# Moving the first layer norm's weight and bias from the residual to the turned tiles

## The chip, the cores and the metric

One core of one Trainium2 chip runs the kernel. The metric is the device time in microseconds (us) of one execution; of several executions the median is given.

## The reference

One decoder layer on 256 tokens of width 2048, all in float32. Three branches are gated, projected and merged; then

```
mix = merged @ w_out
x   = layer_norm(ALPHA * x + mix, ln1_g, ln1_b)
h   = x @ w_up                        # 2048 -> 2 * 5632
...                                   # causal convolution of width 3, silu(a) * b
x   = layer_norm(ALPHA * x + a @ w_down, ln2_g, ln2_b)
```

Only `ln1_g` and `ln1_b`, the weight and bias of the first of these two layer norms, are handled differently by the change.

## The kernel before

Every matrix product runs in three (or, by columns, two) passes: each float32 operand is split into a rounded part ("hi") and a remainder ("lo"). `pieces` streams a weight matrix as 1 MB transfers into two buffers called `raw`, all on the queue of SyncE. A ScalarE copy makes `whi` and a VectorE subtraction makes `wlo`; both live in four staging buffers, and a fifth piece waits until TensorE has finished with the first. `raw` is free again only after the subtraction.

`tok_major` computes tokens by columns. For each of the 16 row blocks of the weights ("k-tiles") it issues three matmuls for each half of the tokens (128 each). The last 512 columns of `w_out` go another way: KEEP = 14 of the 16 k-tiles go to buffers of their own (`khi`, `klo`), are first used for token half 0 alone, and are then gone through again for token half 1. Between those matmuls the first layer norm of half 0 is worked in. `wout_done` is called when a half is complete, and `wout_during` before the end of the second pass, at the moments when `left` k-tiles are still to come.

The layer norm of one half: `ln1_stats` adds the residual and takes mean and variance (VectorE, then a power on GpSimd). `ln1_norm` normalises 512 columns on ScalarE; `ln1_scale` multiplies by the weight on VectorE and adds the bias on GpSimd, with both vectors spread over all partitions in the tile `gb1` (2 MB of transfers); `ln1_fused` does normalisation, weight and bias in two VectorE instructions. `ln1_turn` transposes four 128 x 128 blocks on TensorE into one of two PSUM buffers `ax`, ScalarE copies them as the hi part into `x1T`, and `ln1_low` subtracts on VectorE for the lo part. `x1T` is what the up-projection multiplies, and `x1` keeps the finished rows as the residual for the second layer norm.

The first block of the up-projection, `feat_major_halves`, also runs by token halves. It uses four pieces that `pull()` has fetched beforehand (`up_kept`, two transfers of 1 MB), and calls `between` (`ln1_rest`) ahead of each, where the transposes of half 1 are issued.

TensorE's order is that of the source in the whole kernel. On ScalarE and VectorE a planner of the compiler sets the order from priorities (`hp`) and its own idea of when inputs are there, except inside `ordered`, where these two engines follow the source. Where instructions from outside that region fall between those inside is again the planner's. Each engine then works strictly in the order it was given.

`rstd_of` ends with `nmr`, minus the mean times the reciprocal deviation: one VectorE and one GpSimd instruction. After the up-projection the buffers `x1T0` and `x1T1` are used again: the first for `g2`, weight and bias of the second layer norm, the second for `spare`, a home for two of the last pieces of `w_down`.

The columns `l1g` and `l1b` (weight and bias with one feature per partition) are made at the start of the kernel, in both versions.

Of the kernel before, what the change touches and what calls it, by code (L numbers as in the profile page):

```python
# [8 lines left out]
F32 = mybir.dt.float32  # L9
F32R = mybir.dt.float32r  # L10
U8 = mybir.dt.uint8
AF = mybir.ActivationFunctionType
ALU = mybir.AluOpType
# [3 lines left out]
P = 128  # L17
S = 256
NT = S // P
D = 2048  # L20
KD = D // P
# [9 lines left out]
LEVELS = (64, 32, 16, 8, 4, 2, 1)  # L31
RAW_BUFS = 2
XPAD = 24
KEEP = 14
ENDS = (256, 512)
CROSS = 5
STARTS = ((0, 2), (2, 2), (4, 4), (8, 4), (12, 4))
# [4 lines left out]
def hybrid_layer(  # L42
# [6 lines left out]
    nc = tc.nc  # L49
    ctx.enter_context(tc.manual_schedule(engines={ENG.PE}))  # L50
    x2 = x[0]
    win, wup, wout, wdown = w_in[0], w_up[0], w_out[0], w_down[0]
# [4 lines left out]
    def sub(o, a, b):  # L57
        nc.vector.tensor_tensor(out=o, in0=a, in1=b, op=ALU.subtract)  # L58

    def add(o, a, b):  # L60
        nc.vector.tensor_tensor(out=o, in0=a, in1=b, op=ALU.add)  # L61

    def mul(o, a, b):
        nc.vector.tensor_tensor(out=o, in0=a, in1=b, op=ALU.mult)  # L64

    def stt(o, a, s, b, op0, op1):
        nc.vector.scalar_tensor_tensor(out=o, in0=a, scalar=s, in1=b, op0=op0, op1=op1)  # L67

    def act(o, a, f, **kw):
        nc.scalar.activation(out=o, in_=a, func=f, **kw)  # L70
# [10 lines left out]
    def pieces(w2, col, width, kt_n, big, step, home=None, low=lambda k0: nc.vector):  # L81
        wv = w2.rearrange("(k p) c -> p k c", p=P)
        for b0 in range(0, kt_n, big):
            bn = min(big, kt_n - b0)
            with hp():
                raw = wst.tile([P, bn, width], F32, name="raw", bufs=RAW_BUFS)
                nc.sync.dma_start(out=raw, in_=wv[:, b0:b0 + bn, col:col + width])
            for s0 in range(0, bn, step):
                n = min(step, bn - s0)
                with hp():  # L90
                    hi, lo = (home or stage)(b0 + s0, n, width)
                    split(hi, lo, raw[:, s0:s0 + n, :], low(b0 + s0))
                yield b0 + s0, n, hi, lo
# [115 lines left out]
    def rstd_of(pool, st, want_nmr=True):  # L209
        mv = pool.tile([P, 4], F32, name="ln_mv", bufs=2)  # L210
        nc.vector.bn_aggr(out=mv[:, 0:2], in_=st)  # L211
        nc.vector.tensor_scalar(out=mv[:, 1:2], in0=mv[:, 1:2], scalar1=LN_EPS, scalar2=None, op0=ALU.add)
        nc.gpsimd.tensor_tensor(out=mv[:, 1:2], in0=mv[:, 1:2], in1=mhalf_c, op=ALU.pow)
        if want_nmr:
            nc.vector.tensor_scalar(out=mv[:, 2:3], in0=mv[:, 0:1], scalar1=-1.0, scalar2=None, op0=ALU.mult)
            nc.gpsimd.tensor_tensor(out=mv[:, 2:3], in0=mv[:, 2:3], in1=mv[:, 1:2], op=ALU.mult)
        return mv[:, 0:1], mv[:, 1:2], mv[:, 2:3]

    xpool_cm = tc.tile_pool(name="xpool", bufs=1, side="right", reuse_waits="tile")
# [31 lines left out]
    def bc(t, n):  # L251
        return t.rearrange("p (a b) -> p a b", b=n)
# [85 lines left out]
    tp = ax_tile()  # L338
    nc.tensor.transpose(tp[:, 0:56], vrow, ident[0:56, 0:56])
    nc.vector.tensor_copy(out=vcol, in_=tp[:, 0:56])  # L340
    lbh, normg, pscale, l1g, l1b = (vcol[:, a:b] for a, b in ((0, 8), (8, 16), (16, 24), (24, 40), (40, 56)))
# [19 lines left out]
    for g in range(2):  # L361
        tp = bc(ax_tile(), P)
# [10 lines left out]
    for j in range(2):  # L373
        ps = tok_major(win, 6144 + 512 * j, xT, KD)
# [3 lines left out]
    for t in range(NT):  # L378
# [3 lines left out]
        _, rs, nmr = rstd_of(mix, st)  # L382
# [5 lines left out]
    for j in range(4):  # L388
# [3 lines left out]
        tp = ax_tile()  # L392
# [34 lines left out]
    for j in range(4):  # L427
        ps = feat_major(win, 5120 + 256 * j, xT, KD)
# [259 lines left out]
    ff = ff_cm.__enter__()  # L688
    x1T_h = [ff.tile([P, KD // 2, 2 * S], F32R, name=f"x1T{i}") for i in range(2)]
    x1 = ff.tile([P, NT, D], F32, name="x1")  # L690
    st1 = ff.tile([P, NT, 4, 6], F32, name="st1")
    for j in range(4):
        cs = slice(512 * j, 512 * (j + 1))
# [2 lines left out]
    keep_cm = tc.tile_pool(name="keep", bufs=KEEP // 2, reuse_waits="tile")  # L696
    keep = keep_cm.__enter__()

    gb1 = keep.tile([P, 2, D], F32, name="gb1", bufs=1)
    nc.gpsimd.dma_start(out=gb1[:, 0, :], in_=ln1_g[0].partition_broadcast(P))  # L700
    nc.gpsimd.dma_start(out=gb1[:, 1, :], in_=ln1_b[0].partition_broadcast(P))

    def keep_home(k0, n, width):
        if k0 < KD - KEEP:
            return stage(k0, n, width)
# [2 lines left out]
    ln1_mr = {}  # L708
    ln1_tp = {}

    def ln1_stats(t, ps):
        cs = slice(1536, 2048)
        stt(x1[:, t, cs], x1[:, t, cs], ALPHA, ps, ALU.mult, ALU.add)
        nc.vector.bn_stats(out=st1[:, t, 3, :], in_=x1[:, t, cs])
        ln1_mr[t] = rstd_of(ff, st1[:, t])

    def ln1_fused(t, c):
        mu, rs, _ = ln1_mr[t]
        cs = slice(512 * c, 512 * (c + 1))
        xc = x1[:, t, cs]  # L720
        stt(xc, xc, mu, gb1[:, 0, cs], ALU.subtract, ALU.mult)
        stt(xc, xc, rs, gb1[:, 1, cs], ALU.mult, ALU.add)

    def ln1_norm(t, c):
        _, rs, nmr = ln1_mr[t]
        xc = x1[:, t, 512 * c:512 * (c + 1)]
        act(xc, xc, AF.Identity, scale=rs, bias=nmr)

    def ln1_scale(t, c):
        cs = slice(512 * c, 512 * (c + 1))  # L730
        xc = x1[:, t, cs]
        mul(xc, xc, gb1[:, 0, cs])
        nc.gpsimd.tensor_tensor(out=xc, in0=xc, in1=gb1[:, 1, cs], op=ALU.add)  # L733

    def ln1_turn(t, c):
        tp = bc(ax_tile(), P)
        for j in range(4):
            nc.tensor.transpose(tp[:, j, :], x1[:, t, 512 * c + j * P:512 * c + (j + 1) * P], ident)  # L738
        xh, c4 = x1T_h[c // 2], 4 * (c % 2)
        hi = xh[:, c4:c4 + 4, t * P:(t + 1) * P]  # L740
        act(hi, tp, AF.Copy)
        ln1_tp[t, c] = xh[:, c4:c4 + 4, S + t * P:S + (t + 1) * P], tp, hi.bitcast(F32)

    def ln1_low(t, c):
        sub(*ln1_tp[t, c])

    for j in range(3):
        cs = slice(512 * j, 512 * (j + 1))
        ps = tok_major(wout, 512 * j, mT, KD) if j else first_out
        with hp():  # L750
            for t in range(NT):
                stt(x1[:, t, cs], x1[:, t, cs], ALPHA, ps[t], ALU.mult, ALU.add)
                nc.vector.bn_stats(out=st1[:, t, j, :], in_=x1[:, t, cs])
    up_pieces = pieces(wup, 0, 256, KD, 8, 4, low=lambda k0: nc.vector if k0 < 8 else nc.gpsimd)
    up_kept = []
    up_next = pieces(wup, DFF, 256, KD, 8, 4)
    up_early = []

    def pull():
        up_kept.append(next(up_pieces))  # L760

    ordered = tc.manual_schedule(engines={ENG.Activation, ENG.DVE})

    def wout_done(t, ps, c0, c1):
        with hp(2):
            if t == 0:
                ordered.__enter__()
                ln1_stats(0, ps)
                pull()
                for c in range(4):  # L770
                    ln1_norm(0, c)
                    ln1_scale(0, c)
                pull()
            else:
                ln1_stats(1, ps)
                pull()
                ln1_low(0, 2)
                ln1_low(0, 3)
                ln1_norm(1, 2)
                ln1_norm(1, 3)  # L780
                ln1_fused(1, 0)
                ln1_fused(1, 1)

    def wout_during(c):
        with hp(2):
            ln1_turn(0, c)
            if 0 < c < 3:
                ln1_low(0, c - 1)
            if c == 2:
                pull()  # L790

    tok_major(wout, 1536, mT, KD, last=KEEP, home=keep_home, done=wout_done,
              during={left: [lambda c=c: wout_during(c)] for c, left in enumerate((5, 3, 2, 0))})

    def x1T(k):
        return x1T_h[k // 8][:, k % 8, :]

    def ln1_rest(t, c):
        with hp(2):
            if (t, c) == (0, 3):  # L800
                ln1_turn(1, 0)
                ln1_scale(1, 2)
                ln1_low(1, 0)
                ln1_scale(1, 3)
            elif (t, c) == (1, 0):
                ln1_turn(1, 1)
                ln1_low(1, 1)
            elif (t, c) == (1, 1):
                ln1_turn(1, 2)
                ln1_low(1, 2)  # L810
                ln1_turn(1, 3)
                ln1_low(1, 3)
                up_early.append(next(up_next))
            elif (t, c) == (1, 2):
                up_early.append(next(up_next))
                ordered.__exit__(None, None, None)

    ps_first = feat_major_halves(up_kept, x1T, KD, ln1_rest)
    keep_cm.__exit__(None, None, None)
# [6 lines left out]
    for j in range(KF // 2):  # L826
        ac = []
        for half in range(2):
            if j == 0 and half == 0:
                ps = ps_first  # L830
# [20 lines left out]

    st2 = up.tile([P, NT, 5, 6], F32, name="st2", bufs=1)
    g2 = ff.tile([P, 2, D], F32, name="x1T0")
    spare = ff.tile([P, 2, 4, 512], F32R, name="x1T1")

    def tail_home(k0, n, width):
        if 32 <= k0 < 36:
# [49 lines left out]
    for j in range(3):  # L907
        cs = slice(512 * j, 512 * (j + 1))
        ps = tok_major(wdown, 512 * j, aT, KF)
        if j == 0:  # L910
            nc.gpsimd.dma_start(out=g2[:, 0, :], in_=ln2_g[0].partition_broadcast(P))
            nc.gpsimd.dma_start(out=g2[:, 1, :], in_=ln2_b[0].partition_broadcast(P))
        with hp():
            for t in range(NT):
                stt(x1[:, t, cs], x1[:, t, cs], ALPHA, ps[t], ALU.mult, ALU.add)
                nc.vector.bn_stats(out=st2[:, t, j, :], in_=x1[:, t, cs])
    tok_major(wdown, 1536, aT, KF, last=12, home=tail_home, done=ln2_last, ends=ENDS)
    up_cm.__exit__(None, None, None)
    ff_cm.__exit__(None, None, None)
# [40 lines left out]
```

## Time and profile before

| | |
|---|---|
| median of three runs | 1600.36 us (1599.52 to 1601.9) |
| the profiled execution's own time | 1600.03 us |
| its span, first to last instruction | 1598.3 us |
| TensorE busy | 1578.2 us |
| VectorE, ScalarE, GpSimd busy | 1001.7, 828.8, 48.4 us |
| read from memory | 301.71 MB |
| mean granted TensorE clock | 0.997 of full |

The 1.7 us between span and time lie before the first and after the last instruction. TensorE is busy nearly throughout, so a change moves the time by what TensorE waits, or by the clock it is granted.

### The profile page before, as it was taken

The page shows a single profiled execution, that of the slowest core. Times are in us where ns is not written, and L with a number is a line of the kernel's source. Part 1 is how long each engine was busy: PE and PEld are TensorE (multiplying, and loading weights), DVE is VectorE, ACT ScalarE, POOL GpSimd, SP SyncE. Part 2 cuts the span into 40 slices and gives each one's busy share as a digit, 9 for nine tenths or more (in the row PEclk, how much of TensorE's full clock was granted, in tenths as well). Part 3 has the DMA queues.
Part 4 walks back from the last instruction along what each step waited for, and adds up shares of the span by engine and source line. Part 5 has one row for each costly group of instructions (what it writes and reads, how often), then busy time and mean ns, then how long its engine had stood idle before and what let it go on. Part 6 is the DMA issues. An engine that isn't in the chain of part 4 may idle for free. (4 is left out here: it accounts for less than half of the span.)

```text
span 1598.3 us, 20294 instructions
## 1 busy us (share of the span) xinstructions
PE 1578.2 (99%) x8129; PEld 1344.8 (84%) x8129; DVE 1001.7 (63%) x1196; ACT 828.8 (52%) x962; POOL 48.4 (3%) x116
## 2 busy tenths in 40 slices
PE   9999999999999999999999999999999999999997
PEld 7888888888888887888888888888888888888886
DVE  6666547765448755447567677676676667445455
ACT  5455558546458555444435555555555555333332
POOL 1100000000000001000003000000000000000001
PEclk9999999999999999999999999999999999999999
DMA  7656555655555547655553655555655556655553
GB/s 246 234 185 198 185 191 174 195 178 169 192 189 172 199 160 263 211 186 183 187 208 106 210 186 184 186 191 194 193 184 185 187 192 231 208 185 201 193 186 130
DMA packets 217213, 305.10 MB, mean 191 GB/s; under 512 B 5148, under 2 KB 137812, under 8 KB 216608
## 3 DMA queue, kind: packets, MB, share of 16 engines
q1 hardware_dynamic: 214912, 294.67, 55.8%
q0 software_dynamic: 2208, 9.16, 1.7%
q8 instruction: 63, 1.03, 0.3%
q14 instruction: 30, 0.25, 0.0%
HBM read 301.71 MB, written 2.10 MB: 190 GB/s over the span
## 5 line engine op out<-in xcount | busy, mean ns | idle before, releaser
L74 DVE TENSOR_TENSOR wlo<-raw,whi 128x1024 fp32r<-128x1024 f32 x541 | 659.1, 1222 | 530.4 <-ACT whi L70 529.7
L70 ACT ACTIVATE whi<-raw 128x1024 fp32r<-128x1024 f32 x543 | 571.1, 1056 | 664.2 <-PE mm L151 281.6
L108 PE MATMUL mm<-x1T,whi 128*128 128x512 f32 x1376 | 432.2, 395 | 0.0
L111 PEld LDWEIGHTS mm<-x1T,wlo 128*128 128x128 f32 x1376 | 258.5, 188 | 61.1
L111 PE MATMUL mm<-x1T,wlo 128*128 128x256 f32 x1376 | 270.3, 278 | 0.0
L150 PE MATMUL mm<-wlo,X 128*128 128x512 f32 x612 | 238.4, 389 | 1.3 <-DVE wlo L74 1.3
L149 PE MATMUL mm<-whi,X 128*128 128x512 f32 x612 | 239.5, 391 | 0.0
L151 PE MATMUL mm<-whi,X 128*128 128x512 f32 x612 | 238.2, 389 | 0.0
L108 PEld LDWEIGHTS mm<-x1T,whi 128*128 128x128 f32 x1376 | 209.4, 189 | 0.0
L108 PE MATMUL mm<-X,whi 128*128 128x512 f32 x640 | 201.5, 396 | 0.9 <-DVE X L74 0.9
L111 PEld LDWEIGHTS mm<-X,wlo 128*128 128x128 f32 x640 | 120.2, 188 | 28.4
L150 PEld LDWEIGHTS mm<-wlo,X 128*128 128x128 f32 x612 | 114.9, 188 | 25.1 <-DVE wlo L74 2.0
L149 PE MATMUL mm<-whi,aT 128*128 128x512 f32 (+1 forms) x352 | 135.2, 384 | 0.0
L150 PE MATMUL mm<-wlo,aT 128*128 128x512 f32 (+1 forms) x352 | 135.2, 384 | 0.0
L151 PE MATMUL mm<-whi,aT 128*128 128x512 f32 (+1 forms) x352 | 135.2, 384 | 0.0
L151 PEld LDWEIGHTS mm<-whi,X 128*128 128x128 f32 x612 | 114.9, 188 | 24.1
L149 PEld LDWEIGHTS mm<-whi,X 128*128 128x128 f32 x612 | 114.9, 188 | 23.5 <-ACT whi L70 0.2
L111 PE MATMUL mm<-X,wlo 128*128 128x256 f32 x640 | 125.8, 278 | 0.0
L108 PEld LDWEIGHTS mm<-X,whi 128*128 128x128 f32 x640 | 97.7, 189 | 1.5 <-DVE X L74 1.2
L150 PEld LDWEIGHTS mm<-wlo,aT 128*128 128x128 f32 x352 | 66.1, 188 | 13.2
L151 PEld LDWEIGHTS mm<-whi,aT 128*128 128x128 f32 x352 | 66.1, 188 | 13.1
L149 PEld LDWEIGHTS mm<-whi,aT 128*128 128x128 f32 x352 | 66.1, 188 | 13.0
(189 smaller groups left out, 1281.1 us busy)
## 6 DMA issues: line engine op xcount, KB each, us to landing
raw<-in_w_in_dram SPq DMA_DIRECT2D x102, 1024.0 KB, 5.0
raw<-in_w_up_dram SPq DMA_DIRECT2D x88, 1024.0 KB, 5.1
raw<-in_w_down_dram SPq DMA_DIRECT2D x44, 1024.0 KB, 5.0
raw<-in_w_out_dram SPq DMA_DIRECT2D x16, 1024.0 KB, 5.1
raw<-in_w_pool_proj_dram SPq DMA_DIRECT2D x8, 1024.0 KB, 5.0
raw<-in_w_sg_proj_dram SPq DMA_DIRECT2D x8, 1024.0 KB, 5.1
raw<-in_w_hg_proj_dram SPq DMA_DIRECT2D x8, 1024.0 KB, 5.0
x<-in_x_dram POOLq DMA_DIRECT2D x4, 512.0 KB, 7.6
```

What stands on the lines that cost most here:

```text
L70: nc.scalar.activation(out=o, in_=a, func=f, **kw)
L74: low.tensor_tensor(out=lo, in0=src, in1=hi.bitcast(F32), op=ALU.subtract)
L108: nc.tensor.matmul(ps[:, c, :], lhsT=hi[:, k, c * P:(c + 1) * P], rhs=xT(kt)[:, 0:512], start=kt == 0, stop=False)
L111: nc.tensor.matmul(ps[:, c, 0:256], lhsT=lo[:, k, c * P:(c + 1) * P], rhs=xT(kt)[:, 0:256], start=False, stop=kt == kt_n - 1)
L149: nc.tensor.matmul(o[:, w], lhsT=xT(kt)[:, xs], rhs=hi[:, k, w], start=kt == first, stop=False)
L150: nc.tensor.matmul(o[:, w], lhsT=xT(kt)[:, xs], rhs=lo[:, k, w], start=False, stop=False)
L151: nc.tensor.matmul(o[:, w], lhsT=xT(kt)[:, xl], rhs=hi[:, k, w], start=False, stop=kt == kt_n - 1)
```

## The change

- `KEEP` is 16: all k-tiles of the last block of `w_out` are kept, and the first pass serves token half 0 alone from the start. `gb1` no longer lies beside them.
- `ln1_norm` normalises all eight pieces of 512 columns on ScalarE, and `x1` then holds the normalised rows without weight and bias. `ln1_scale` and `ln1_fused` go.
- `ln1_turn` applies weight and bias after the transpose: four ScalarE instructions for the hi part and four VectorE instructions into a new tile `full`, one each per 128 x 128 block, and one subtraction for the lo part. Everything of a turn is emitted together.
- All four `pull()` of the first up block are emitted before `ordered` begins, and all four of their subtractions are VectorE's; two were GpSimd's.
- The turns of half 0 come at 7, 5, 3 and 1 k-tiles left; those of half 1 two at once ahead of the last piece of half 0, then one ahead of each of the first two pieces of half 1.
- `nmr` is one VectorE instruction.
- `gb1` is loaded at the start of the down-projection into `x1T1`, and `x1` is multiplied and added there, 16 VectorE instructions on 128 x 512. `spare` is taken afterwards.

```diff
-KEEP = 14
+KEEP = 16
...
         if want_nmr:
-            nc.vector.tensor_scalar(out=mv[:, 2:3], in0=mv[:, 0:1], scalar1=-1.0, scalar2=None, op0=ALU.mult)
-            nc.gpsimd.tensor_tensor(out=mv[:, 2:3], in0=mv[:, 2:3], in1=mv[:, 1:2], op=ALU.mult)
+            nc.vector.tensor_scalar(out=mv[:, 2:3], in0=mv[:, 0:1], scalar1=mv[:, 1:2], scalar2=-1.0, op0=ALU.mult,
+                                    op1=ALU.mult)
...
-    gb1 = keep.tile([P, 2, D], F32, name="gb1", bufs=1)
-    nc.gpsimd.dma_start(out=gb1[:, 0, :], in_=ln1_g[0].partition_broadcast(P))
-    nc.gpsimd.dma_start(out=gb1[:, 1, :], in_=ln1_b[0].partition_broadcast(P))
...
+        full = bc(keep.tile([P, 512], F32, name="full", bufs=2), P)
+        for j in range(4):
+            k = 4 * c + j
+            g, b = l1g[:, k:k + 1], l1b[:, k:k + 1]
+            act(xh[:, c4 + j, t * P:(t + 1) * P], tp[:, j, :], AF.Identity, scale=g, bias=b)
+            nc.vector.tensor_scalar(out=full[:, j, :], in0=tp[:, j, :], scalar1=g, scalar2=b, op0=ALU.mult, op1=ALU.add)
         hi = xh[:, c4:c4 + 4, t * P:(t + 1) * P]
-        act(hi, tp, AF.Copy)
...
+        sub(xh[:, c4:c4 + 4, S + t * P:S + (t + 1) * P], full, hi.bitcast(F32))
...
-    up_pieces = pieces(wup, 0, 256, KD, 8, 4, low=lambda k0: nc.vector if k0 < 8 else nc.gpsimd)
+    up_pieces = pieces(wup, 0, 256, KD, 8, 4)
...
             if t == 0:
+                for _ in range(4):
+                    pull()
                 ordered.__enter__()
-                ln1_stats(0, ps)
-                pull()
-                for c in range(4):
-                    ln1_norm(0, c)
-                    ln1_scale(0, c)
-                pull()
...
+            ln1_stats(t, ps)
+            for c in range(4):
+                ln1_norm(t, c)
...
-              during={left: [lambda c=c: wout_during(c)] for c, left in enumerate((5, 3, 2, 0))})
+              during={left: [lambda c=c: wout_during(c)] for c, left in enumerate((7, 5, 3, 1))})
...
             if (t, c) == (0, 3):
                 ln1_turn(1, 0)
...
+                ln1_turn(1, 1)
+            elif t == 1 and c < 2:
+                ln1_turn(1, 2 + c)
+            elif t == 1:
                 up_early.append(next(up_next))
...
-    spare = ff.tile([P, 2, 4, 512], F32R, name="x1T1")
+    gb1 = ff.tile([P, 2, D], F32, name="x1T1")
+    nc.gpsimd.dma_start(out=gb1[:, 0, :], in_=ln1_g[0].partition_broadcast(P))
+    nc.gpsimd.dma_start(out=gb1[:, 1, :], in_=ln1_b[0].partition_broadcast(P))
+    for c in range(4):
+        cs = slice(512 * c, 512 * (c + 1))
+        for t in range(NT):
+            mul(x1[:, t, cs], x1[:, t, cs], gb1[:, 0, cs])
+            add(x1[:, t, cs], x1[:, t, cs], gb1[:, 1, cs])
...
+    spare = ff.tile([P, 2, 4, 512], F32R, name="x1T1")
     tok_major(wdown, 1536, aT, KF, last=12, home=tail_home, done=ln2_last, ends=ENDS)
```

## Rows read from the trace of the kernel before

**Rows 1.** First part of the page: busy time, share, instructions.
```profile
PE 1578.2 (99%) x8129; PEld 1344.8 (84%) x8129; DVE 1001.7 (63%) x1196; ACT 828.8 (52%) x962; POOL 48.4 (3%) x116
```

**Rows 2.** Waits of TensorE, whole span: total us, times, longest.
```profile
PE ax L738 <- issue: 1.9, 1, 1.9
...
PE mm L150 <- DVE wlo L74: 1.3, 2, 0.8
PE ax L738 <- POOL x L733: 1.2, 1, 1.2
```

**Rows 3.** Windows: length, busy of each engine, granted clock, DMA share, GB/s.
```profile
847.00:850.40 3.40, 3.40 (x15) 2.73 (x12) 0.73 (x2) 1.55 (x2) 1.55 (x2) 0.54 0.94 305
821.90:867.80 45.90, 42.37 (x257) 37.07 (x256) 33.66 (x42) 20.24 (x25) 17.18 (x14) 0.96 0.35 115
```

**Rows 4.** Timeline of TensorE, 820 to 868: start, us, what, idle before.
```profile
821.91 0.39 PE L149 MATMUL mm<-whi,X 128*128 128x512 f32 x1
...
840.04 0.39 PE L151 MATMUL mm<-khi,X 128*128 128x512 f32 x1
...
846.72 0.63 PE L738 MATMUL ax<-id,x 128*128 128x128 f32 x4 [1.94 <-issue]
...
850.36 0.53 PE L132 MATMUL mm<-x1T,whi 128*128 128x256 f32 x1
...
867.80 0.68 PE L108 MATMUL mm<-x1T,whi 128*128 128x512 f32 x2
```

**Rows 5.** Timelines of ScalarE and VectorE, 827 to 853.
```profile
827.28 2.01 ACT L70 ACTIVATE khi<-raw 128x1024 fp32r<-128x1024 f32 x2 [2.70 <-DMA raw<-in_w_out_dram]
838.17 2.93 ACT L70 ACTIVATE x<-x,ln_mv 128x512 f32<-128x512 f32 x4 [5.01 <-POOL ln_mv L216]
...
852.73 1.52 ACT L70 ACTIVATE x<-x,ln_mv 128x512 f32<-128x512 f32 x2 [0.44 <-POOL ln_mv L216]
...
828.37 2.36 DVE L74 TENSOR_TENSOR klo<-raw,khi 128x1024 fp32r<-128x1024 f32 x2 [1.52 <-ACT khi L70]
834.35 0.69 DVE L67 SCALAR_TENSOR_TENSOR x<-x,mm 128x512 f32<-128x512 f32 x1 [3.61 <-PE mm L151]
...
849.89 0.69 DVE L67 SCALAR_TENSOR_TENSOR x<-x,mm 128x512 f32<-128x512 f32 x1 [2.67 <-PE mm L151]
```

**Rows 6.** The page's DMA issues: count, KB each, median us to landing.
```profile
raw<-in_w_up_dram SPq DMA_DIRECT2D x88, 1024.0 KB, 5.1
```

**Rows 7.** Timelines of SyncE's queue, VectorE and ScalarE, 866 to 876.
```profile
866.65 0.37 SPq L87 DMA_DIRECT2D raw<-in_w_up_dram  x1
...
870.24 0.68 DVE L61 TENSOR_TENSOR h<-mm,fm_low 128x512 f32<-128x512 f32 x1
...
873.18 1.06 ACT L70 ACTIVATE whi<-raw 128x1024 fp32r<-128x1024 f32 x1 [3.63 <-DMA raw<-in_w_up_dram]
874.15 1.08 ACT L70 ACTIVATE cv<-h,ccol 128x256 f32<-128x256 f32 x2
```

**Rows 8.** Groups by line and shape: count, busy us, mean ns, idle before.
```profile
L70 ACT ACTIVATE cv<-h,ccol 128x256 f32<-128x256 f32 x88 | 47.5, 586 | 1.4 <-DVE h L61 1.4
L70 ACT ACTIVATE x<-x,ln_mv 128x512 f32<-128x512 f32 x8 | 5.9, 784 | 21.9 <-DVE x L67 16.4 <-POOL ln_mv L216 5.4
L70 ACT ACTIVATE x1T<-ax 128x512 fp32r<-128x512 f32 x8 | 4.8, 599 | 12.4 <-PE ax L738 12.4
L394 DVE COPY ccol<-ax 128x88 f32<-128x88 f32 x4 | 0.8, 220 | 0.5 <-PE ax L393 0.5
```

**Rows 9.** Timeline of TensorE at 627, and `gb1`'s second transfer (us to landing).
```profile
627.15 0.50 PE L150 MATMUL mm<-wlo,X 128*128 128x512 f32 x1 [0.75 <-DVE wlo L74]
...
gb<-in_ln_b_dram POOLq DMA_DIRECT2D x1, 1024.0 KB, 9.9
```

**Rows 10.** Timelines of TensorE and VectorE where the down-projection begins.
```profile
1347.16 0.40 PE L149 MATMUL mm<-whi,aT 128*128 128x512 f32 x1
...
1353.53 1.23 DVE L74 TENSOR_TENSOR wlo<-raw,whi 128x1024 fp32r<-128x1024 f32 x1 [0.75 <-ACT whi L70]
```

More of the change, by code (lines that the diff above doesn't have):

```diff
@@ L715, in ln1_stats @@
         ln1_mr[t] = rstd_of(ff, st1[:, t])
[L717 to L722, printed above, removed]
     def ln1_norm(t, c):
@@ L727, in ln1_norm @@
         act(xc, xc, AF.Identity, scale=rs, bias=nmr)
[L729 to L733, printed above, removed]
     def ln1_turn(t, c):
@@ L739, in ln1_turn @@
         xh, c4 = x1T_h[c // 2], 4 * (c % 2)
+        full = bc(keep.tile([P, 512], F32, name="full", bufs=2), P)
[4 more added lines that the diff above has]
+            nc.vector.tensor_scalar(out=full[:, j, :], in0=tp[:, j, :], scalar1=g, scalar2=b, op0=ALU.mult, op1=ALU.add)
         hi = xh[:, c4:c4 + 4, t * P:(t + 1) * P]
-        act(hi, tp, AF.Copy)
-        ln1_tp[t, c] = xh[:, c4:c4 + 4, S + t * P:S + (t + 1) * P], tp, hi.bitcast(F32)
-    def ln1_low(t, c):
-        sub(*ln1_tp[t, c])
+        sub(xh[:, c4:c4 + 4, S + t * P:S + (t + 1) * P], full, hi.bitcast(F32))
     for j in range(3):
@@ L766, in wout_done @@
             if t == 0:
+                for _ in range(4):
+                    pull()
                 ordered.__enter__()
-                ln1_stats(0, ps)
-                pull()
-                for c in range(4):
-                    ln1_norm(0, c)
-                    ln1_scale(0, c)
-                pull()
[L774 to L782, printed above, removed]
+            ln1_stats(t, ps)
+            for c in range(4):
+                ln1_norm(t, c)
     def wout_during(c):
@@ L786, in wout_during @@
             ln1_turn(0, c)
[L787 to L790, printed above, removed]
     tok_major(wout, 1536, mT, KD, last=KEEP, home=keep_home, done=wout_done,
-              during={left: [lambda c=c: wout_during(c)] for c, left in enumerate((5, 3, 2, 0))})
+              during={left: [lambda c=c: wout_during(c)] for c, left in enumerate((7, 5, 3, 1))})
     def x1T(k):
@@ L801, in ln1_rest @@
                 ln1_turn(1, 0)
[L802 to L805, printed above, removed]
                 ln1_turn(1, 1)
[L807 to L812, printed above, removed]
+            elif t == 1 and c < 2:
+                ln1_turn(1, 2 + c)
+            elif t == 1:
                 up_early.append(next(up_next))
-            elif (t, c) == (1, 2):
-                up_early.append(next(up_next))
-                ordered.__exit__(None, None, None)
+                if c == 3:
+                    ordered.__exit__(None, None, None)
     ps_first = feat_major_halves(up_kept, x1T, KD, ln1_rest)
```

## The prediction

> **What bounds the kernel.** I read the busy shares first: TensorE works through 99% of the span [rows 1], and the change gives it the same matmuls and the same 32 transposes as before. So only TensorE's waits and its clock can move the time. Next come its waits [rows 2]. Apart from start and end the kernel has few: two ahead of transposes in the layer norm (1.2 and 1.9 us), and two on a late `wlo` (together 1.3 us). The windows [rows 3] then show the layer norm's stage, from the first matmul of `w_out`'s last block (821.9) to the second up block (867.8): 45.9 us, TensorE busy in 42.4 of them. The stretch from 847.0 to 850.4 had a granted clock of 0.54, nearly the lower of the two levels, 1.2 instead of 2.4 GHz. It follows the wait of 1.9 us that ended at 846.72 [rows 4]. At full clock its work would have fitted into 3.40 x 0.54 = 1.84 us, so the slow clock cost about 1.6 us. The stage without waits and at full clock takes 45.9 - 3.5 - 1.6 = 40.8 us. More than 5.1 us can't be won here; the question is which waits come back.
>
> **When the first pass ends.** From 821.91 to 840.04 there are 80 matmul starts [rows 4], 0.227 us each. After the change the first pass is 16 k-tiles of three matmuls for half 0: it ends at 821.9 + 48 x 0.227 = 832.8, some 1.4 us earlier, and the second pass is as much longer. The first turn stands nine k-tiles later, as it did: 832.8 + 27 x 0.227 = 838.9. Its input must be normalised by then.
>
> **The path to the first turn.** From the residual addition on VectorE to the first normalisation on ScalarE it took 834.35 to 838.17, 3.8 us [rows 5]. The merged `nmr` saves one hop and changes little. Then comes one `ln1_norm`, 0.8 us [rows 8]; weight and bias are no longer between it and the transpose, and the wait on GpSimd (1.2 us) loses its cause. If the statistics start at 832.9, the turn is ready just before 838.9.
>
> **What may stand in front.** The four splits of the first up block are now emitted ahead of the statistics, with the highest priority, and outside the ordered region: the planner places them. They need two transfers. The second could be issued once the last `klo` was through, at 828.37 + 2.36 = 830.7 [rows 5]. That chain (buffer free, transfer, split) begins at a piece staged as before, so I keep 830.7; the first two k-tiles now go to kept buffers and free the other `raw` sooner (an estimate: the six matmuls that no longer come first, 1.4 us), which bounds the gain here. With 5.1 us to landing [rows 6] it is there at 835.8. Two splits take from ScalarE's start at 827.28 to 830.73 on VectorE, 3.45 us [rows 5], so the last `wlo` ends at 839.3. If the planner puts these subtractions before the statistics, VectorE, working in order, holds up the statistics behind them, and with these all normalisations and turns.
>
> Does it? Rows show that the planner expects transfers too early. A transfer issued at 866.65 was still awaited by ScalarE at 873.18, for 3.6 us, while the `cv` instructions queued behind that split had their input at 870.9 [rows 7]. The planner had thus reckoned with at most 4.3 us where the chip took 6.5. Three such transfers follow each other up to ours, so in the plan the piece is ready about when the first pass ends, and at a tie the higher priority wins. I take it that both subtractions stand in front. Then the statistics start at 839.3, the first normalisation at 843.1, and the turn at 843.9: TensorE waits 4.9 us at one place. Two shorter waits [rows 2] brought the clock down before, so I count the 1.6 us once more (bounds 0 and 1.6).
>
> **The turns.** No row shows a 128-wide ScalarE instruction with scale and bias per partition. The nearest have 512 and 256 columns, 0.784 and 0.586 us, which on a line give 0.49 for 128; two of 256 columns took 1.08 us, so they start 0.49 apart [rows 7, 8], 0.1 less than one lasts. Four take 4 x 0.39 + 0.1 = 1.65 us against 0.60 for the one copy. Bounds: 0.6 (no dearer than the copy) and 4 x 0.59 = 2.4. On VectorE the nearest from PSUM is 0.22 for 88 columns: about 0.26 each, four 1.0, then the subtraction; ScalarE stays the longer. A normalisation starts every 0.73 us [rows 5]. Half 0: ScalarE follows each turn in 1.65 us where TensorE brings one every 1.8 (two k-tiles and a transpose), so no wait. Half 1: the halves of the first up block took 850.36 to 867.80 for 32 k-tile steps, 0.5 us each with their transposes [rows 4], so turn (1,0) comes some 5.6 us after the pass. The chain before it is the end of turn (0,3), 2.8 us from the residual addition to the first normalisation (849.89 to 852.73 [rows 5]) and 0.8 for that, about in time. Turn (1,2) must wait until ScalarE has done two more normalisations and turn (1,0) and so freed a PSUM buffer, and the first piece of half 1 for its lo part: 0.9 us together (bounds 0 and 2.5).
>
> The Trainium skill ("VectorE: DVE Perf Modes", section "The TRN2 errata — SBUF-src ops pay a fixed extra latency per instruction") speaks against four small instructions: the fixed cost is paid for each, and it advises 512 elements or more. By its ScalarE figure for a PSUM source an estimate for 128 columns is 0.25 us, a turn 1.0 instead of 1.65, which takes the 0.9 us of late waits away and puts my forecast at 1600.5. No row here shows that shape.
>
> **Early and late transfers.** The 1.3 us of waits on `wlo` fall at 627 (0.75 us) and soon after, behind `gb1`, whose second half took 9.9 us to landing, twice what a weight transfer takes [rows 2, 6, 9]. Without `gb1` I expect both gone: -1.3 (bounds 0 and -1.3). The 2 MB now fall where the down-projection begins, after the last up matmul (1347.16). There the fifth piece was split at 1353.53 and is needed after four pieces of 12 matmuls: 1347.16 + 48 x 0.227 = 1358.1 [rows 10]; its `wlo` was done at 1354.8, with 3.3 us to spare. The burst's own delay of a piece lies under that, so I put 0 (bound: the 1.3 it cost before). The 16 VectorE instructions are some 0.69 us each [rows 5], 11 us, inside a block of 264 matmuls, 60 us, in which VectorE has one subtraction of 1.23 us for every 2.7 us of TensorE: nothing, if they don't block. In GpSimd's queue the two transfers wait for the last up matmul; behind them stand at most the two of `g2`, which nobody needs before the second layer norm, and `spare` is free once the additions are through, 150 us before its use. Two subtractions that were GpSimd's are in the 3.45 us above, and the two normalisations that ScalarE gains are in its chain. The other `nmr`, of the gating unit, is far from any wait of TensorE: nothing.
>
> **The sum.** 40.8 + 4.9 + 1.6 + 0.9 = 48.2 us against 45.9: +2.3. With -1.3 early: +1.0. The profiled execution took 1600.03 us, 0.33 below the median of the runs; against the median the forecast is 1601.4.
>
> **Rivals.**
> - *The statistics are not held up.* If the plan has the transfers no earlier than the chip, the statistics come first, the turn is ready at 838.6, and ScalarE (busy with the two splits until 837.9) is just in time. No wait at the first turn, but half 1 comes sooner relative to ScalarE's backlog, and its waits grow to about 2.3: 40.8 + 2.3 = 43.1, -2.8, with the early -1.3 it is 1596.3. Against it: the planner's early guess [rows 7].
> - *Only the end of the statistics is late.* Mean and variance pass while VectorE waits for the second transfer, but `nmr`, now VectorE's, falls behind the subtractions: normalisation at 839.5, turn at 840.3, a wait of 1.4 and late waits of 2.0, no slow clock: 44.2, -1.7 - 1.3: 1597.4.
> - *The late `gb1` holds VectorE (slower).* The planner, too early again, puts the additions of the bias ahead of weight pieces. If the bias lands 10.8 us after an issue at 1347.8 (the longest transfer of the earlier burst took 9.9), an addition runs at 1358.6 to 1359.3 and the fifth piece's `wlo` ends at 1360.5, 2.4 us late; with a fallen clock 4 us on top of the forecast: 1605.5. It decides once VectorE is held past 1356.8. The Trainium skill ("SBUF — State Buffer", section "SBUF: two separate sides") adds that a transfer issued by GpSimd can starve for descriptors while VectorE holds the shared port, which would make such a landing later still; no run shows it here.
>
> **Chances and range.** Forecast 0.50, statistics free 0.18, `nmr` alone 0.15, late `gb1` 0.17. About 0.2% (3.2 us) is what a measurement of this kernel can tell from no change. Faster than 1597.2: most of the second case and some of the third, 0.21. Slower than 1603.6: the fourth and the upper edge of the first, 0.23. Same: 0.56. The forecast's own range is 1598.9 (no slow clock, no late waits) to 1603.0 (late waits at their bound). Eight in ten reach from 1596.0 to 1604.8.
>
> **What would show it.** Right: a wait of 4 to 5 us ahead of the first transposes near 839, VectorE idle before a `wlo` near 836 with the residual addition behind it, a stretch at half clock after it, no wait of TensorE near 627. Wrong: the residual addition at 833; TensorE waiting for a `wlo` between 1355 and 1365; or four ScalarE instructions of a turn far from 1.65 us.

## The result, and the profile after

The changed kernel takes 1617.64 us (median of five) against 1599.52 us before (also five): a ratio of 1.011, with a 95% interval of 1.0098 to 1.0122. Four of its executions lie between 1615.61 and 1619.66 us; the fifth was slow, at 2262.93 us with a mean granted clock of 0.653, and the ratio leaves it out. The forecast was 1601.4, the range up to 1604.8: it missed by 16 us. The profiled execution took 1617.64 us, with a span of 1615.9 us.

The first part of the page and TensorE's waits over the whole span, the lines that answer to [rows 1, 2]:

```profile
PE 1585.6 (98%) x8129; PEld 1351.7 (84%) x8129; DVE 1014.8 (63%) x1236; ACT 839.2 (52%) x988; POOL 31.3 (2%) x104
```

```profile
PE ax L721 <- ACT x L70: 9.0, 2, 5.2
PE mm L132 <- DVE x1T L58: 3.1, 4, 1.8
PE ax L721 <- DVE full L728: 2.7, 3, 1.1
```

The matmuls are as many as before, but they are 7.4 us longer busy, and 14.8 us of waits have appeared where the layer norm had 3.4 us before, in all three rows at something of the layer norm. The waits on `wlo` that cost 1.3 us before [rows 2] are gone.

Windows of three stretches in the layer norm's stage, and then of the whole stage (length; busy time of TensorE, its weight loads, VectorE, ScalarE and GpSimd, each with its number of instructions; granted clock, DMA share, GB/s):

```profile
842.30:848.10 5.80, 5.73 (x18) 4.75 (x19) 1.66 (x5) 4.21 (x9) 0.00 (x0) 0.50 0.16 53
863.90:868.60 4.70, 4.64 (x22) 4.64 (x23) 1.14 (x3) 3.39 (x7) 0.00 (x0) 0.50 0.01 3
879.00:885.50 6.50, 5.59 (x28) 5.43 (x27) 5.27 (x7) 3.75 (x5) 0.00 (x0) 0.50 0.03 5
821.40:885.54 64.14, 49.37 (x257) 43.06 (x256) 37.39 (x66) 30.52 (x51) 1.20 (x4) 0.84 0.26 83
```

The stage took 45.9 us before [rows 3] and takes 64.1 now: 18.2 us more, against 17.6 us more of the whole span. Everything else together is 0.6 us shorter. So the loss lies in this stage alone. Three stretches at a granted clock of 0.50, the lower level of 1.2 GHz, have 16.0 us of matmuls in them and cost half of that, 8.0 us; the waits are 14.8; and 40.8 + 14.8 + 8.0 = 63.6 of the 64.1. The forecast had the same 40.8, then 5.8 of waits and 1.6 of clock.

TensorE's timeline (start, length, what ran, in brackets the idle time ahead of it and what ended that), against [rows 4]:

```profile
842.37 1.12 PE L721 MATMUL ax<-id,x 128*128 128x128 f32 x4 [3.81 <-ACT x L70]
851.97 0.65 PE L721 MATMUL ax<-id,x 128*128 128x128 f32 x4 [1.13 <-DVE full L728]
...
863.96 1.97 PE L721 MATMUL ax<-id,x 128*128 128x128 f32 x8 [5.16 <-ACT x L70]
...
873.55 0.66 PE L721 MATMUL ax<-id,x 128*128 128x128 f32 x4 [1.02 <-DVE full L728]
...
878.23 0.36 PE L132 MATMUL mm<-x1T,whi 128*128 128x256 f32 x1 [1.84 <-DVE x1T L58]
...
885.54 0.83 PE L108 MATMUL mm<-x1T,whi 128*128 128x512 f32 x2
```

The first wait, 3.81 us ahead of the first turn, is the one that was forecast. The others were not: 5.16 us ahead of half 1's turns, three waits for a PSUM buffer, and waits for the lo part of `x1T`. Two of the slow stretches, at 842.3 and 863.9, begin where the waits of 3.81 and 5.16 us end. The third, from 879.0, follows the wait of 1.84 us that ended at 878.23.

Now the two engines that work on a turn. VectorE's timeline, against [rows 5]:

```profile
836.40 2.36 DVE L74 TENSOR_TENSOR wlo<-raw,whi 128x1024 fp32r<-128x1024 f32 x2 [1.36 <-ACT whi L70]
838.68 0.68 DVE L67 SCALAR_TENSOR_TENSOR x<-x,mm 128x512 f32<-128x512 f32 x1
...
844.82 0.41 DVE L728 TENSOR_SCALAR full<-ax,vcol 128x128 f32<-128x128 f32 x1 [3.35 <-ACT x1T L70]
845.76 0.41 DVE L728 TENSOR_SCALAR full<-ax,vcol 128x128 f32<-128x128 f32 x1 [0.53 <-ACT x1T L70]
846.70 0.41 DVE L728 TENSOR_SCALAR full<-ax,vcol 128x128 f32<-128x128 f32 x1 [0.53 <-ACT x1T L70]
847.63 0.41 DVE L728 TENSOR_SCALAR full<-ax,vcol 128x128 f32<-128x128 f32 x1 [0.53 <-ACT x1T L70]
848.08 0.69 DVE L58 TENSOR_TENSOR x1T<-full,x1T 128x512 fp32r<-128x512 f32 x1
848.69 0.40 DVE L728 TENSOR_SCALAR full<-ax,vcol 128x128 f32<-128x128 f32 x1
...
859.68 0.69 DVE L58 TENSOR_TENSOR x1T<-full,x1T 128x512 fp32r<-128x512 f32 x1
860.29 0.68 DVE L67 SCALAR_TENSOR_TENSOR x<-x,mm 128x512 f32<-128x512 f32 x1
```

ScalarE's timeline over the same turn:

```profile
841.51 2.93 ACT L70 ACTIVATE x<-x,ln_mv 128x512 f32<-128x512 f32 x4 [4.19 <-DVE ln_mv L215]
844.34 0.44 ACT L70 ACTIVATE x1T<-ax,vcol 128x128 fp32r<-128x128 f32 x1
845.26 0.46 ACT L70 ACTIVATE x1T<-ax,vcol 128x128 fp32r<-128x128 f32 x1 [0.48 <-DVE full L728]
846.20 0.46 ACT L70 ACTIVATE x1T<-ax,vcol 128x128 fp32r<-128x128 f32 x1 [0.48 <-DVE full L728]
```

Laid side by side, the two never overlap. ScalarE's second block runs from 845.26 to 845.72, VectorE's from 845.76 to 846.17, ScalarE's third starts at 846.20. Each waits for the other: 0.46 + 0.41 and two handovers of some 0.035 us make 0.94 us a block. From the first VectorE block of one turn (844.82) to that of the next (848.69) it is 3.87 us, where the forecast had 1.65. Nothing in the data asks for it: ScalarE writes `x1T`, VectorE writes `full`, and both only read `ax`. The waits of 838 to 886 us, both ways:

```profile
DVE full L728 <- ACT x1T L70: 19.4, 26, 3.3
ACT x1T L70 <- DVE full L728: 15.7, 24, 1.2
```

What follows can be read down VectorE's timeline. It works all four turns of half 0 at that pace, ends them at 860.3, and only then comes half 1's residual addition; its pass had been done at 853.1, where the first up matmul stands. The path from the addition to the first normalisation is 2.8 us (860.29 to 863.10), so turn (1,0), due at 858.8, stands at 863.96. The kernel before had the subtractions of the last two turns behind half 1's statistics; by emitting everything of a turn together, the change put them ahead. Before the change the second reader waited too, but unavoidably: the subtraction needs ScalarE's result, and there was one handover a turn.

The Trainium skill ("PSUM — Partial Sum Buffer", section "PSUM bank collisions raise a hardware error") states the rule that I had not weighed: the compiler adds a dependency between any two instructions on different engines that touch the same bank on the same partitions, two reads included; the chip, it says, does not arbitrate. The trace agrees, with these 26 and 24 waits between two readers. Whether the rule goes by the bank or by the buffer, no run here separates.

### The profile page after: what moved, and what is told of

Its sections match the earlier page's. It is cut to its first block, busy times and chain, and to the rows that moved or that the text cites. A ratio compares the mean times of both kernels' runs of the same rounds, so it can differ in the third digit from the quotient of the medians.

```text
span 1615.9 us, 20341 instructions
## 1 busy us (share of the span) xinstructions
PE 1585.6 (98%) x8129; PEld 1351.7 (84%) x8129; DVE 1014.8 (63%) x1236; ACT 839.2 (52%) x988; POOL 31.3 (2%) x104
## 4 chain that ended last, share of the span: by engine, by line
PE 94%; DVE 2%; issue 1%; DMA 1%; ACT 1%; SPq 0%; POOL 0%; ACTq 0%; POOLq 0%
PE mm L108 29%; PE mm L151 16%; PE mm L150 16%; PE mm L149 16%; PE mm L111 15%; PE ax L547 1%; DMA raw<-in_w_out_dram 1%; DMA acc<-in_w_in_dram 1%; DVE full L728 0%; ACT x1T L70 0%; DVE x L67 0%; DMA raw<-in_w_up_dram 0%; DVE wlo L74 0%; DVE klo L74 0%; PE ax L509 0%
## 5 line engine op out<-in xcount | busy, mean ns | idle before, releaser
L151 PE MATMUL mm<-whi,X 128*128 128x512 f32 x608 | 236.6, 389 | 0.0
L151 PE MATMUL mm<-whi,aT 128*128 128x512 f32 (+1 forms) x352 | 135.2, 384 | 0.0
L151 PEld LDWEIGHTS mm<-whi,X 128*128 128x128 f32 x608 | 114.1, 188 | 23.8
L151 PEld LDWEIGHTS mm<-whi,aT 128*128 128x128 f32 x352 | 66.2, 188 | 13.0
```

What stands on the lines that cost most here:

```text
L151: nc.tensor.matmul(o[:, w], lhsT=xT(kt)[:, xl], rhs=hi[:, k, w], start=False, stop=kt == kt_n - 1)
```

## The experiments

The first theory (A): the two readers' turn-taking sets the length of a turn, and the late statistics add a few us. The rival (B): the statistics that stand behind the planner's splits are the cause, by their wait, the slow clock and the late half 1. A second rival (C): the small instructions are themselves too dear, whatever their order. Four kernels beside 21 runs of the kernel before, 1599.92 us.

**e1_grouped**: the same eight instructions, in two groups.

```diff
         for j in range(4):
             k = 4 * c + j
-            g, b = l1g[:, k:k + 1], l1b[:, k:k + 1]
-            act(xh[:, c4 + j, t * P:(t + 1) * P], tp[:, j, :], AF.Identity, scale=g, bias=b)
-            nc.vector.tensor_scalar(out=full[:, j, :], in0=tp[:, j, :], scalar1=g, scalar2=b, op0=ALU.mult, op1=ALU.add)
+            act(xh[:, c4 + j, t * P:(t + 1) * P], tp[:, j, :], AF.Identity, scale=l1g[:, k:k + 1], bias=l1b[:, k:k + 1])
+        for j in range(4):
+            k = 4 * c + j
+            nc.vector.tensor_scalar(out=full[:, j, :], in0=tp[:, j, :], scalar1=l1g[:, k:k + 1], scalar2=l1b[:, k:k + 1],
+                                    op0=ALU.mult, op1=ALU.add)
```

> Alternation (the two readers of one PSUM buffer take turns block by block, 0.94 us a block, 3.9 us a turn): with ScalarE's four instructions together and then VectorE's four, a turn takes some 2 to 2.5 us and the time falls to about 1603 us (1601 to 1606). Small instructions (128 columns are dear by themselves, whoever reads): no change, 1616 to 1618. Late statistics (the 4 us before the first turn and what follows make the loss): no change, 1616 to 1618.

Measured: 1603.03 us, ratio 1.0024 (1.0013 to 1.0035). Nothing is done less or elsewhere, one handover a turn takes the place of seven, and 15 of the 18 us are gone. The two timelines, ScalarE's lines and then VectorE's:

```profile
842.50 1.48 ACT L70 ACTIVATE x1T<-ax,vcol 128x128 fp32r<-128x128 f32 x4
844.59 1.51 ACT L70 ACTIVATE x1T<-ax,vcol 128x128 fp32r<-128x128 f32 x4 [0.60 <-PE ax L721]
```

```profile
844.02 1.37 DVE L729 TENSOR_SCALAR full<-ax,vcol 128x128 f32<-128x128 f32 x4 [4.39 <-ACT x1T L70]
845.42 0.69 DVE L58 TENSOR_TENSOR x1T<-full,x1T 128x512 fp32r<-128x512 f32 x1
846.13 1.37 DVE L729 TENSOR_SCALAR full<-ax,vcol 128x128 f32<-128x128 f32 x4
```

VectorE still doesn't begin until ScalarE has left the buffer (842.50 + 1.48 = 843.98), but then the next turn's ScalarE work runs in the other buffer beside it: 2.11 us a turn instead of 3.87. Four in a row take 1.48 and 1.37, not four times 0.46 and 0.41: the alternation also takes away the overlap of one instruction with the next. That decides against C. VectorE is now the longer of the two, by its subtraction: 2.0 to 2.1 us a turn against 1.5 for ScalarE.

**e2_one_reader**: only VectorE reads PSUM; ScalarE makes the hi part from `full`.

```diff
-            act(xh[:, c4 + j, t * P:(t + 1) * P], tp[:, j, :], AF.Identity, scale=g, bias=b)
...
         hi = xh[:, c4:c4 + 4, t * P:(t + 1) * P]
+        act(hi, full, AF.Copy)
```

> VectorE alone reads PSUM and makes the full-precision tile; ScalarE takes the rounded part from it with one copy of 512 columns. Alternation: a turn is some 2 us of VectorE's time, the time about 1602 us (1600 to 1605). Small instructions: half of them are gone, about 1609. Late statistics: 1616 to 1618.

Measured: 1602.57 us, 1.0017 (1.0007 to 1.0026). One reader is as good as two that are grouped. A turn takes VectorE 2.67 us, since it waits for ScalarE's copy between its own two steps.

**e3_stats_first**: the alternation stays, the splits go behind the statistics.

```diff
             if t == 0:
-                for _ in range(4):
-                    pull()
                 ordered.__enter__()
             ln1_stats(t, ps)
+            if t == 0:
+                pull()
+                pull()
             for c in range(4):
                 ln1_norm(t, c)
+            if t == 0:
+                pull()
+                pull()
```

> The statistics of half 0 stand ahead of the splits of the first up block. Alternation: everything after them starts 5 to 6 us sooner but the turns keep 3.9 us each, about 1612 us. Late statistics: nearly all of the 17 us comes back, about 1602. Small instructions: about 1612.

Measured: 1614.16 us, 1.0086 (1.0069 to 1.0103). Two rows of TensorE's timeline:

```profile
843.14 1.12 PE L721 MATMUL ax<-id,x 128*128 128x128 f32 x4 [2.56 <-DVE full L728]
...
859.00 1.97 PE L721 MATMUL ax<-id,x 128*128 128x128 f32 x8 [5.14 <-ACT x L70]
```

The first turn no longer waits, but a later one waits 2.56 us for a buffer that the alternation holds, and half 1 is as late as before, 5.14 us. Against the kernel before it is 14.2 us slower, so B is worth some 3.5 to 4 of the 18 us, less than the forecast of 1612 gave it.

**e4_two_banks**: the interleaved loop, but each engine reads a buffer of its own. It does work that the kernel doesn't: the transposes are made twice.

```diff
-        tp = bc(ax_tile(), P)
-        for j in range(4):
-            nc.tensor.transpose(tp[:, j, :], x1[:, t, 512 * c + j * P:512 * c + (j + 1) * P], ident)
+        tp, tq = bc(ax_tile(), P), bc(ax_tile(), P)
+        for to in (tp, tq):
+            for j in range(4):
+                nc.tensor.transpose(to[:, j, :], x1[:, t, 512 * c + j * P:512 * c + (j + 1) * P], ident)
...
-            nc.vector.tensor_scalar(out=full[:, j, :], in0=tp[:, j, :], scalar1=g, scalar2=b, op0=ALU.mult, op1=ALU.add)
+            nc.vector.tensor_scalar(out=full[:, j, :], in0=tq[:, j, :], scalar1=g, scalar2=b, op0=ALU.mult, op1=ALU.add)
```

> Each turn transposes twice, into both PSUM buffers, and each engine reads its own; 32 more transposes, some 3 us of TensorE. Alternation: the four and four instructions run beside each other, a turn takes 1.7 us, about 1604 us (1602 to 1608). Small instructions: 3 us dearer than the changed kernel, 1619 to 1621. Late statistics: the same, 1619 to 1621.

Measured: 1603.87 us, 1.0027 (1.0017 to 1.0037), the 32 added transposes included. ScalarE's timeline and VectorE's:

```profile
841.79 1.48 ACT L70 ACTIVATE x1T<-ax,vcol 128x128 fp32r<-128x128 f32 x4
```

```profile
841.64 1.37 DVE L729 TENSOR_SCALAR full<-ax,vcol 128x128 f32<-128x128 f32 x4 [2.72 <-PE ax L722]
```

Same instructions, same order in the source: with a buffer each, the two engines run beside each other from 841.8 to 843.0. It is the shared buffer, and not the order, the engines or their instructions, that makes them take turns. The forecast's picture of a turn was that of this kernel, though even here VectorE's four instructions and its subtraction (1.37 + 0.69) are longer than ScalarE's four.

Four more, beside 27 runs of the kernel before, 1599.46 us. What is left once the alternation is gone, and can the change be made to pay?

**e5_one_reader_stats** and **e6_grouped_stats** put e3's edit on e2 and on e1.

> VectorE as the only reader of PSUM, and the statistics ahead of the splits. If late statistics cost what the trace of the run with one reader shows (3.9 us at the first turn and a stretch at half clock, 1.6), it comes out 4 to 5 us below that run's 1602.6: about 1598. If VectorE's chain (2.7 us a turn) sets the end anyway, the gain is given back: 1601 to 1603.

Measured: 1600.07 us, 1.0003 (0.9994 to 1.0012), between the two that were expected.

> Grouped readers, and the statistics ahead of the splits. Late statistics cost 3.7 us at the first turn and the slow clock after it in the run with grouped readers: 4 to 5 us below its 1603.0, about 1598.5. If VectorE, with 2.0 us a turn after ScalarE's, holds the second half's statistics instead, 1601 to 1603.

Measured: 1599.36 us, 0.9998 (0.999 to 1.0007). With both causes taken away the change costs nothing, and gains nothing either. Each against its own runs of the kernel before, the changed kernel loses 18.1 us, e1 3.1 and e6 none: grouping the readers takes away 15.0 us, and the earlier statistics the other 3.2. What still waits in e6 is mostly half 1 (3.2 of 4.0 us): its statistics start at 847.88, right behind VectorE's last instruction of turn (0,3):

```profile
845.87 1.36 DVE L729 TENSOR_SCALAR full<-ax,vcol 128x128 f32<-128x128 f32 x4
847.27 0.69 DVE L58 TENSOR_TENSOR x1T<-full,x1T 128x512 fp32r<-128x512 f32 x1
847.88 0.68 DVE L67 SCALAR_TENSOR_TENSOR x<-x,mm 128x512 f32<-128x512 f32 x1
```

**e7_act_reader**: ScalarE alone reads PSUM and writes `full` (four buffers); VectorE makes both parts from it later, those of turns (0,2) and (0,3) behind half 1's statistics. The statistics of half 0 come first, as in e3.

```diff
-            g, b = l1g[:, k:k + 1], l1b[:, k:k + 1]
-            act(xh[:, c4 + j, t * P:(t + 1) * P], tp[:, j, :], AF.Identity, scale=g, bias=b)
-            nc.vector.tensor_scalar(out=full[:, j, :], in0=tp[:, j, :], scalar1=g, scalar2=b, op0=ALU.mult, op1=ALU.add)
+            act(full[:, j, :], tp[:, j, :], AF.Identity, scale=l1g[:, k:k + 1], bias=l1b[:, k:k + 1])
+        ln1_tp[t, c] = full
+
+    def ln1_low(t, c):
+        xh, c4, full = x1T_h[c // 2], 4 * (c % 2), ln1_tp[t, c]
         hi = xh[:, c4:c4 + 4, t * P:(t + 1) * P]
+        nc.vector.tensor_copy(out=hi, in_=full)
         sub(xh[:, c4:c4 + 4, S + t * P:S + (t + 1) * P], full, hi.bitcast(F32))
...
             ln1_stats(t, ps)
...
+            else:
+                ln1_low(0, 2)
+                ln1_low(0, 3)
             for c in range(4):
                 ln1_norm(t, c)
```

> ScalarE as the only reader of PSUM: four instructions make the full-precision tile, VectorE copies the rounded part and subtracts (some 1.0 us a turn instead of 2.0), its part of the last two turns of half 0 stands behind the second half's statistics, and the first half's statistics come ahead of the splits. By the sum of the prediction (40.8 us of work in the stage, 1.3 us won early) nearly all waits go: 1594 to 1596. If turns cost what the small instructions cost whoever reads, no better than 1598.

Measured: 1592.15 us (1591.37 to 1593.53), 0.9956 (0.9943 to 0.9968): 7.3 us faster than the kernel before, 25 faster than the changed one, and some 2 below what was expected. TensorE's wait in the stage, a window of it (columns as above), and VectorE's timeline:

```profile
PE mm L132 <- DVE x1T L58: 0.4, 2, 0.3
```

```profile
820.00:862.00 42.00, 41.56 (x264) 37.04 (x263) 27.93 (x42) 28.99 (x53) 1.20 (x4) 1.00 0.40 130
```

```profile
830.30 0.69 DVE L67 SCALAR_TENSOR_TENSOR x<-x,mm 128x512 f32<-128x512 f32 x1 [2.17 <-PE mm L151]
...
839.38 0.43 DVE L732 CAST x1T<-full 128x512 fp32r<-128x512 f32 x1
839.84 0.69 DVE L58 TENSOR_TENSOR x1T<-full,x1T 128x512 fp32r<-128x512 f32 x1
...
843.04 0.69 DVE L67 SCALAR_TENSOR_TENSOR x<-x,mm 128x512 f32<-128x512 f32 x1 [1.12 <-PE mm L151]
```

Both residual additions now start as soon as TensorE's pass is done (`<-PE mm L151`), TensorE waits 0.4 us in the stage, and the clock stays at 1.00. ScalarE's line shows three turns without a gap:

```profile
837.87 4.27 ACT L70 ACTIVATE full<-ax,vcol 128x128 f32<-128x128 f32 x12
```

The stage runs from 819.22 to 860.15: 40.9 us, the 40.8 that the forecast put down for its work without waits. It is 5.0 us shorter than before [rows 3], and in the profiled execution it begins 2.7 us earlier (821.91 before), where the forecast had 1.3 for the early gain. How the gain over e5 divides between the reader and the later lo parts, no run separates.

**e8_before_pulls**: the kernel before, with one part of the change alone: the four `pull()` stand ahead of `ordered` and all subtractions are VectorE's.

> The kernel before, with nothing changed but that the four splits of the first up block are emitted ahead of the ordered region, all subtractions VectorE's. If the planner's order makes the statistics late by itself, TensorE waits 4 to 6 us ahead of the first transposes and the time rises to 1604 to 1607. If lateness comes from another part of the change, it stays at 1600.

Measured: 1602.89 us, 1.0018 (1.0009 to 1.0027): 3.4 us slower, in the direction of the first case and short of its 1604 to 1607. VectorE's timeline, then a row of TensorE's:

```profile
839.13 2.36 DVE L74 TENSOR_TENSOR wlo<-raw,whi 128x1024 fp32r<-128x1024 f32 x2 [3.44 <-ACT whi L70]
841.41 0.68 DVE L67 SCALAR_TENSOR_TENSOR x<-x,mm 128x512 f32<-128x512 f32 x1
```

```profile
847.68 1.11 PE L738 MATMUL ax<-id,x 128*128 128x128 f32 x4 [7.05 <-POOL x L733]
```

The splits stand in front of the statistics here too, after 3.44 us in which VectorE did nothing. The wait of 7.05 us is longer than expected; in this execution the last split of `w_out` also began later, at 829.32 against 827.28 before [rows 5], after 4.93 us of waiting for its transfer. So the trace shows the order, and how much of the wait it costs is uncertain by that delay. A row of TensorE's waits in the same kernel settles the early gain:

```profile
PE mm L150 <- DVE wlo L74: 1.3, 2, 0.8
```

With `gb1` loaded early it is there; in none of the kernels that load it late is there one on that line for a `wlo`. The stage begins at 821.7 and 821.9 in the two traces that load `gb1` early, and at 818.9 to 821.4 in the eight that load it late.

## Why the prediction was wrong

**The step that failed: "The turns".** It took ScalarE's four instructions and VectorE's four to run beside each other, and wrote "ScalarE stays the longer". From that came 1.65 us a turn, with 2.4 as the upper bound. Measured: 3.87 us, because the two engines share `ax` and each read waits for the other engine's. The price of one ScalarE instruction was nearly right: 0.46 us for the guessed 0.49, and four in a row 1.48 for 1.65. On VectorE one took 0.41 for 0.26. The sum of the two engines, with handovers, was never formed, and the upper bound left out what two readers of one buffer cost. "ScalarE stays the longer" failed by itself as well: the forecast's own numbers give VectorE 1.0 for the four and 0.69 for a subtraction, 1.7 us, and with the reads grouped it took 2.0. In the trace of before, ScalarE's copy and VectorE's subtraction from the same `ax` follow each other by their data, so no row showed the rule; the source shows the two readers of `tp` one line apart.

**What hung on it.** "Turn (1,0) ... about in time" rested on half 0's turns ending early on VectorE: the wait was 5.16 us. The late waits, 0.9 with a bound of 2.5, came to 11.0 (14.8 less the first 3.81), and the clock fell three times, 8.0 us instead of 1.6.

**"What may stand in front" was right.** The subtractions stood ahead of the statistics: the residual addition at 838.68 (forecast 839.3), VectorE idle for 1.36 us ahead of the `wlo` at 836.40. The size was a little less: the first normalisation at 841.51 for 843.1, the wait 3.81 for 4.9, because the path from statistics to normalisation took 2.8 us and not 3.8. GpSimd's power is the difference, in the trace before (half 0) and in the one after:

```profile
836.33 1.53 POOL L213 TENSOR_TENSOR ln_mv<-ln_mv,cc 128x1 f32<-128x1 f32 x1 [222.51 <-DVE ln_mv L215]
```

```profile
840.66 0.56 POOL L213 TENSOR_TENSOR ln_mv<-ln_mv,cc 128x1 f32<-128x1 f32 x1 [233.02 <-DVE ln_mv L212]
```

Why it took 1.53 us there, no run shows; for half 1 of the kernel before it took 0.55. The half-clock stretch behind the wait came, and was longer than forecast: 5.7 us of matmuls at half clock, 2.9 us instead of 1.6. That step alone costs 3.4 us (e8), or 3.2 between e1 and e6. A slip beside it: with statistics at 832.9 the forecast has the turn ready "just before 838.9", but its own terms give 832.9 + 3.8 + 0.8 = 837.5. The two rivals in which the statistics or most of them go free fall with it; e6 shows what the first would have been, with turns grouped: 1599.4, not 1596.3.

**The other steps.** The two early waits (1.3 us together) went, but the stage of the changed kernel begins only 0.5 us earlier in its trace (821.40): in the first 200 us of that execution TensorE waited 0.5 us longer than before, and its granted clock was 0.99 instead of 1.00. The late `gb1` is hidden, and its rival is refuted; VectorE's timeline in the down-projection:

```profile
1373.17 1.23 DVE L74 TENSOR_TENSOR wlo<-raw,whi 128x1024 fp32r<-128x1024 f32 x1 [2.51 <-ACT whi L70]
...
1376.65 1.29 DVE L64 TENSOR_TENSOR x<-x,x1T 128x512 f32<-128x512 f32 x2
...
1380.39 1.29 DVE L61 TENSOR_TENSOR x<-x,x1T 128x512 f32<-128x512 f32 x2
```

The first multiplications and additions come at 1376.65 and 1380.39, behind the fifth piece, whose `wlo` (first row) was done at 1374.40, and TensorE has no wait after 890. The margin was smaller than forecast: ScalarE waited 2.95 us for that piece's transfer, and the `wlo` came 1.5 us ahead of its use (1365.05 + 48 x 0.227 = 1375.9), where the forecast had 3.3. The end of the first pass stands too: e7's statistics begin 11.1 us after the stage does, as 832.8 was forecast from 821.9. And e1, which is the change without the alternation, is 3.1 us slower than the kernel before, where the forecast had 1.0 and the upper end of its own range 2.6. In e1's trace the first wait is 3.7 us, the later ones are 3.4, and TensorE is busy for 44.4 us of the stage, 3.6 more than 40.8. So the rest of the account held in kind, but even without the alternation its late waits (0.9) and its clock (1.6) were priced 4.5 us too low together; a shorter first wait and an earlier start of the stage give about half of that back.

**The rule on small instructions.** By its fixed cost for a PSUM source the Trainium skill ("VectorE: DVE Perf Modes", section "The TRN2 errata — SBUF-src ops pay a fixed extra latency per instruction") gave an estimate of 0.25 us for 128 columns on ScalarE. The trace differs, 0.46 alone and 0.34 from start to start in a row, for instructions with scale and bias per partition; the measurement decides. Its advice against small instructions agrees with the rows: four in a row took 1.48 us (e1) where one copy of 512 columns took 0.60 [rows 8]. In e7, where ScalarE has the time for them, TensorE waits only 0.4 us in the stage.

**Left open.** Whether the chip would have served both readers at once was not tried: it would mean taking a wait away. The Trainium skill ("PSUM — Partial Sum Buffer", section "PSUM bank collisions raise a hardware error") says that two engines on one bank at once raise an error; no run here shows that.

## What to carry to other kernels

Before pricing instructions as running side by side, list for each PSUM buffer who reads it: here ScalarE and VectorE, reading one buffer, took turns, instruction by instruction, in the order of the source, though neither wrote it. Group each engine's reads, give each a buffer, or let one engine empty the buffer and the other work from its copy. And ask what is queued behind the engine that now takes turns: here 5.2 us of waits stood ahead of the second half's turns, whose statistics were queued behind it, and 6.4 us of the loss were the clock.

## What the runs showed of the hardware

- Two readers of one PSUM buffer: 0.94 us for a 128 x 128 block on ScalarE and on VectorE in alternation (0.46 + 0.41 + two handovers of 0.035), 1.48 and 1.37 us for four blocks at a time, and these beside each other where each engine has its own buffer.
- Back to back, a 128-wide instruction from PSUM starts 0.34 us after the one before it on ScalarE ((1.48 - 0.46) / 3) and 0.32 us on VectorE ((1.37 - 0.41) / 3), so an engine that is made to wait between them loses more than the wait.
- The wait of 1.84 us that ended at 878.23 was followed by matmuls at full clock up to about 879, and then by 6.5 us at 1.2 GHz (879.0 to 885.5, granted clock 0.50). In this stage the clock cost 8.0 us beside 14.8 us of waits, and 1.6 beside 3.4 in the kernel before.
